# A decoder layer in split precision: position biases folded into a scale, the side branch's loads moved behind other copies, the last tile cut elsewhere, a shorter reciprocal root

## The chip, the core and the metric

One core of a Trainium2 chip runs the whole kernel. TensorE (PE) multiplies matrices and transposes; VectorE (DVE), ScalarE (ACT) and GpSimd (POOL) do the elementwise work; SyncE (SP) issues most transfers. The metric is the device time of one execution in microseconds.

## The reference

One hybrid layer on 512 tokens of width 1024, all in float32: block-sparse attention with position slopes (8 heads of 64) beside chunked retention (4 heads of 128), a gated feed-forward part with a convolution over three tokens, a side branch of `p` (width 256) under a gate, and a last norm. With 512 tokens there are two blocks of 256 keys and every earlier block is chosen, so the attention is plain causal attention.

```python
def rmsnorm(x, g):
    ms = jnp.mean(x * x, axis=-1, keepdims=True)
    return x * lax.rsqrt(ms + RMS_EPS) * g
...
h = rmsnorm(x, attn_norm[i])
mq, mk, mv, rq, rk, rv, rg = jnp.split(h @ w_in[i], split_points, axis=-1)
moba_out = ...   # softmax(q k^T * 64**-0.5 - 2**-(head+1) * distance) v, causal
ret_out = head_groupnorm(ret, ret_norm[i]) * jax.nn.silu(rg)
x = x + jnp.concatenate([moba_out, ret_out], axis=-1) @ w_out[i]
h = rmsnorm(x, ffn_norm[i])
u = causal_dwconv(h @ w_up[i], conv_w[i], conv_b[i])
x = x + (jax.nn.gelu(u) * (h @ w_gate[i])) @ w_down[i]
g = jax.nn.sigmoid(rmsnorm(x, ple_norm[i]) @ w_ple_gate[i])
x = x + (p[i] @ w_ple[i]) * g
return rmsnorm(x, final_norm)
```

## The kernel before

**Products.** Each float32 product is made from three (`mm3`, L91 to L95): both factors are split into a rounded part (`...h`) and the rest (`...l`), and high × high, high × low and low × high add up in one accumulator. The moving side has 512 columns nearly everywhere. Tiles of 128 × 512 come from a heap of 76 buffers (`h2k`), so a new tile can be made to wait for the last reader of an old one.

**Weights.** The SP queue loads blocks of 1 MB into one of two buffers `wr` (`fetch`, L125 to L134). `prepare` has ScalarE write the high part `wh` (L152) and VectorE or, for the weights of the projections and of the output product, POOL subtract to the rest `wl` (L154). It runs one part ahead of the products that use it (`need`).

**Order.** TensorE's instructions run in the order in which the code issues them (L846 to L853 add a dependence from each to the next). The order on the other engines is set by a scheduler of the framework.

**Stages.** The first norm and the retention values (to 34 us); projections and retention (to about 157 us); the attention loop (L646 to L671, to about 262 us); the feed-forward part (to 654 us); the last stage (to 701 us).

**The attention loop.** Heads are taken in pairs `g`, and each pair in two blocks of queries `b`. `moba_scores` makes the scores `ms` in PSUM and calls `softmax`: VectorE adds the bias and finds the least value (`ml`, L458), ScalarE takes the exponential with its sum (`me`, `mt`, L461), VectorE the reciprocal (`mi`), and one of them scales. `moba_turn` transposes the probabilities (`mp`), and ScalarE and VectorE split them into `corner` or `mph` and `mpl` (L515, L516). `moba_values` multiplies by the values (`mo`, L525 and L526), with small steps `mr`, `mt`, `mxh` behind it. Projections, halves of the output product (`ou`) and products of the side branch (`pw`) fill the gaps (`fills`). The heads of the query and key projections `mq` and `mk` are moved to their partitions by transfers from SBUF to SBUF, here called the copies (L380 and L389).

**The side branch.** `ple_load` (L572 to L580) issues four loads `wpr` of `w_ple` and two `pn` of `p`, 256 KB each; `ple_weights` (L589 to L594) splits the weights, with `wpl` on POOL.

**Roots.** `rsqrt_of` (L238 to L256) makes a reciprocal root on VectorE by an integer shift and three Newton steps. It is used for the norms (`r1`, `rr`, `r2`, `r3`: four columns) and for each of the last tiles (`r4`: one column).

**The last stage.** Gate weights are split into `wgh` and `wgl` by VectorE. For each half `c` of the columns and each tile `t` of 128 tokens come the gate product `pg` (24 products of 512 columns), and in `finish` (L788 to L803) the sigmoid `sg`, its product `sm` with `pw`, the residual sum `x`, the square with its sum (`fsq`, `fm`) and the product `x3n` with the last norm's weights on POOL. In the second half the root `r4` and the output `o` follow (L828 to L843). The last tile is cut in two parts of columns, and its `o` is made with the norm's weights in one step.

## Time and profile before

| | us |
|---|---|
| median of three runs | 699.3 (698.32 to 701.1) |
| the profiled execution | 702.57 |
| its span, first to last instruction | 700.8 |

Busy in that span: TensorE 682.7 us (97%), VectorE 428.2 (61%), ScalarE 291.1 (42%), POOL 124.3 (18%). Matmuls are pipelined, so their recorded durations overlap; the distance from one start to the next is what a product costs. In a timeline the figure in square brackets is the idle time of that engine just before the instruction, with what ended it. The mean granted clock is 0.997 of full speed.

### The profile page before, as it was taken

The numbers are of one execution on the slowest core, as the hardware profiler recorded it, in microseconds if no ns is written. First come the engines' busy times: TensorE is split into PE (matmuls) and PEld (weight loads), VectorE is DVE, ScalarE is ACT, GpSimd is POOL, SyncE is SP. The second block draws the span as 40 slices with busy tenths as digits, with TensorE's granted clock in tenths as the row PEclk, the third lists the DMA queues.
The fourth block names the chain that finished last, engine by engine and source line by source line (L and its number), as shares of the span: only waits on it lengthen the run. The fifth ranks groups of instructions, "written<-read, shape, count | busy, mean of one in ns | idle before, by whom it ended". The sixth has DMA issues, their size and how long they took to land.

```text
span 700.8 us, 8440 instructions
## 1 busy us (share of the span) xinstructions
PE 682.7 (97%) x3200; PEld 568.7 (81%) x3200; DVE 428.2 (61%) x769; ACT 291.1 (42%) x476; POOL 124.3 (18%) x99
## 2 busy tenths in 40 slices
PE   8999999999989999999999999999999999999995
PEld 6888888888777878888888888888888888888884
DVE  4676677766657656775656653234565565466496
ACT  4525543326657864453433431222343343344311
POOL 5145344334515210000000000000000000000145
PEclk9999999999999999999999999999999999999998
DMA  8245342236764011232331222233323212344003
GB/s 258 107 120 135 95 117 75 61 92 178 222 180 110 1 62 61 62 119 77 104 121 61 90 90 91 91 120 121 101 79 121 73 63 75 115 149 158 1 1 120
DMA packets 73390, 71.38 MB, mean 102 GB/s; under 512 B 2450, under 2 KB 62726, under 8 KB 73350
## 3 DMA queue, kind: packets, MB, share of 16 engines
q1 hardware_dynamic: 73190, 70.58, 33.3%
q8 instruction: 25, 0.41, 0.3%
q10 hardware_dynamic: 160, 0.27, 0.1%
q14 instruction: 15, 0.12, 0.1%
HBM read 62.97 MB, written 2.10 MB: 93 GB/s over the span
## 4 chain that ended last, share of the span: by engine, by line
PE 89%; DVE 4%; DMA 3%; ACT 1%; issue 1%; POOL 1%; SPq 0%; DVEq 0%; ACTq 0%; POOLq 0%
PE gate L93 6%; PE gate L94 6%; PE up L94 6%; PE dn L93 6%; PE dn L94 6%; PE gate L95 6%; PE up L95 6%; PE up L93 6%; PE dn L95 6%; PE pj L93 4%; PE pj L94 4%; PE pj L95 4%; PE ou L93 2%; PE ou L94 2%; PE ou L95 2%; PE pg L94 1%
## 5 line engine op out<-in xcount | busy, mean ns | idle before, releaser
L152 ACT ACTIVATE wh<-wr 128x1024 fp32r<-128x1024 f32 (+2 forms) x108 | 105.2, 979 | 204.5 <-PE dn L94 60.1
L154 DVE TENSOR_TENSOR wl<-wr,wh 128x1024 fp32r<-128x1024 f32 (+2 forms) x78 | 84.6, 1086 | 45.0 <-ACT wh L152 44.9
L154 POOL TENSOR_TENSOR wl<-wr,wh 128x1024 fp32r<-128x1024 f32 x30 | 73.3, 2444 | 129.9 <-ACT wh L152 129.8
L93 PE MATMUL gate<-h2h,wh 128*128 128x512 f32 x176 | 68.7, 390 | 0.0
L95 PE MATMUL gate<-h2h,wl 128*128 128x512 f32 x176 | 68.5, 389 | 0.0
L94 PE MATMUL gate<-h2l,wh 128*128 128x512 f32 x176 | 68.5, 389 | 0.0
L93 PE MATMUL up<-h2h,wh 128*128 128x512 f32 x176 | 68.5, 389 | 0.0
L94 PE MATMUL up<-h2l,wh 128*128 128x512 f32 x176 | 68.5, 389 | 0.0
L95 PE MATMUL up<-h2h,wl 128*128 128x512 f32 x176 | 68.5, 389 | 0.0
L93 PE MATMUL dn<-ach,wh 128*128 128x512 f32 x176 | 68.5, 389 | 0.0
L94 PE MATMUL dn<-acl,wh 128*128 128x512 f32 x176 | 68.5, 389 | 0.0
L95 PE MATMUL dn<-ach,wl 128*128 128x512 f32 x176 | 68.5, 389 | 0.0
L93 PE MATMUL pj<-h1h,wh 128*128 128x512 f32 x160 | 63.4, 396 | 1.1 <-DVE ml L458 0.9
L95 PE MATMUL pj<-h1h,wl 128*128 128x512 f32 x160 | 62.4, 390 | 0.0
L94 PE MATMUL pj<-h1l,wh 128*128 128x512 f32 x160 | 62.4, 390 | 0.0
L714 POOL MEMSET u<- 128x2 f32 x22 | 2.1, 99 | 316.9 <-DVE c L721 316.9
L725 DVE TENSOR_TENSOR ga<-gate,r2b 128x512 f32<-128x512 f32 x22 | 15.2, 691 | 41.3 <-PE gate L95 41.3
L715 DVE TENSOR_TENSOR u<-up,r2b 128x512 f32<-128x512 f32 x22 | 15.1, 691 | 40.1 <-PE up L95 40.1
L93 PEld LDWEIGHTS up<-h2h,wh 128*128 128x128 f32 x176 | 33.0, 188 | 6.9
L95 PEld LDWEIGHTS dn<-ach,wl 128*128 128x128 f32 x176 | 33.0, 188 | 6.9
L93 PEld LDWEIGHTS dn<-ach,wh 128*128 128x128 f32 x176 | 33.0, 188 | 6.9
L95 PEld LDWEIGHTS gate<-h2h,wl 128*128 128x128 f32 x176 | 33.0, 188 | 6.9
(235 smaller groups left out, 1416.8 us busy)
## 6 DMA issues: line engine op xcount, KB each, us to landing
wr<-in_w_up_dram SPq DMA_DIRECT2D x11, 1024.0 KB, 5.3
wr<-in_w_gate_dram SPq DMA_DIRECT2D x11, 1024.0 KB, 5.3
wr<-in_w_in_dram SPq DMA_DIRECT2D x20, 512.0 KB, 4.0
wr<-in_w_down_dram SPq DMA_DIRECT2D x8, 768.0 KB, 4.2
wr<-in_w_down_dram SPq DMA_DIRECT2D x8, 640.0 KB, 4.1
wr<-in_w_ple_gate_dram SPq DMA_DIRECT2D x4, 1024.0 KB, 5.2
wr<-in_w_out_dram SPq DMA_DIRECT2D x3, 1024.0 KB, 6.2
xn<-in_x_dram SPq DMA_DIRECT2D x8, 256.0 KB, 6.0
```

The costliest lines, as they stand in the source:

```text
L93: nc.tensor.matmul(acc, a[0], b[0], start=first, stop=False)
L94: nc.tensor.matmul(acc, a[0], b[1], start=False, stop=False)
L95: nc.tensor.matmul(acc, a[1], b[0], start=False, stop=last)
L152: nc.scalar.activation(hi, part, AF.Copy)
L154: (nc.gpsimd if aside else nc.vector).tensor_tensor(lo, part, f(hi), op=ALU.subtract)
L714: nc.gpsimd.memset(u[:, 0:2], 0.0)
L715: nc.vector.tensor_tensor(u[:, 2:], up, r2b, op=ALU.mult)
L725: nc.vector.tensor_tensor(ga, gate, r2b, op=ALU.mult)
```

## The change

It has five parts. Line numbers of the changed kernel are a little higher: L154, L156, L398, L407, L475, L479, L524, L542, L585, L588 and L602 are L152, L154, L380, L389, L461, L465, L515, L533, L576, L579 and L593 of before.

1. The eight tiles `bias` made by POOL are gone. The query heads are scaled by a column `qscale` that holds 64**-0.5 × 2**(h+1), and `softmax` reads the unscaled `base` and multiplies the sum by −2**−(h+1).
2. `ple_load` is issued at the end of step 2 of the loop, no longer at the end of step 1, and behind the last SP instruction; `ple_weights` is issued ahead of `moba_values` in its step.
3. The last tile is cut at column 384 where it was cut at 256.
4. `x3n` is made by VectorE.
5. The root takes nine instructions for four columns where it took twelve, and seven for one column where it took nine.

```diff
     def rsqrt_of(v, n, s):
-        sh = sm(s + "s", n, I32)
-        nc.vector.tensor_scalar(sh, v.bitcast(I32), 1, None, op0=ALU.logical_shift_right)
+        c = 1.5 ** 0.2
+        a = c ** (1 / 3)
         half = sm(s + "f", n)
         nc.vector.tensor_scalar(half, v, -0.5, None, op0=ALU.mult)
         y0 = sm(s + "y", n, I32)
-        nc.vector.tensor_scalar(y0, sh, -1.0, float(0x5F3759DF), op0=ALU.mult, op1=ALU.add)
-        y = y0.bitcast(F32)
-        for i in range(3):
+        nc.vector.tensor_scalar(y0, v.bitcast(I32), -0.5, float(0x5F3759DF) + math.log2(a) * 2 ** 23, op0=ALU.mult,
+                                op1=ALU.add)
+
+        def square(y):
             t = sm(s + "t", n)
...
-            y2 = sm(s + "y", n)
-            nc.vector.scalar_tensor_tensor(y2, t, 1.5, y, op0=ALU.add, op1=ALU.mult)
-            y = y2
-        return y
+            return t
+
+        y = y0.bitcast(F32)
+        t = square(y)
+        y1 = sm(s + "y", n)
+        nc.vector.scalar_tensor_tensor(y1, t, 1.5 * a ** 2, y, op0=ALU.add, op1=ALU.mult)
+        t = square(y1)
+        w = sm(s + "t", n)
+        nc.vector.scalar_tensor_tensor(w, t, 5 / 3 * c ** 2, t, op0=ALU.add, op1=ALU.mult)
+        y2 = sm(s + "y", n)
+        nc.vector.scalar_tensor_tensor(y2, w, 1.25 * c ** 4, y1, op0=ALU.add, op1=ALU.mult)
+        return y2
...
+    qscale = const.tile([P, HM // 2], F32, name="qscale")
+    for h in range(HM):
+        nc.gpsimd.memset(qscale[h % 2 * DH:(h % 2 + 1) * DH, h // 2:h // 2 + 1], DH ** -0.5 * 2.0 ** (h + 1))
...
-        nc.vector.scalar_tensor_tensor(t, acc, DH ** -0.5 if name == "mq" else 1.0, r1b, op0=ALU.mult, op1=ALU.mult)
+        nc.vector.scalar_tensor_tensor(t, acc, qscale[:, i:i + 1] if name == "mq" else 1.0, r1b, op0=ALU.mult,
+                                       op1=ALU.mult)
...
-    def moba_bias(h):
-        biases[h] = h2k("bias")
-        nc.gpsimd.tensor_scalar(biases[h], base, 2.0 ** -(h + 1), None, op0=ALU.mult)
...
-        nc.vector.tensor_tensor_reduce(e, s[:, :keys], biases[h][:, T - keys:], scale=-1.0,
+        nc.vector.tensor_tensor_reduce(e, s[:, :keys], base[:, T - keys:], scale=-2.0 ** -(h + 1),
                                        scalar=3.4e38, op0=ALU.add, op1=ALU.min, accum_out=least)
...
+        if 3 <= i < 7:
+            ple_weights((i - 3) // 2, (i - 3) % 2)
         if i >= 2:
             moba_values((i - 2) // 2, i % 2)
...
-        if i == 1:
-            ple_load()
-        if 3 <= i < 7:
-            ple_weights((i - 3) // 2, (i - 3) % 2)
+        if i == 2:
+            with tc.issue_after(last_of(mybir.EngineType.SP)):
+                ple_load()
...
-            nc.gpsimd.tensor_tensor(yn, y, fn[c], op=ALU.mult)
+            nc.vector.tensor_tensor(yn, y, fn[c], op=ALU.mult)
...
-            cuts = [(0, 256), (256, T)] if (t, c) == (NT - 1, 1) else [(0, T)]
+            cuts = [(0, 384), (384, T)] if (t, c) == (NT - 1, 1) else [(0, T)]
```

The change also moves instructions that it doesn't name. A name's number only tells buffers apart.

The SP queue in the attention loop, before, about 177 to 190 us: `wr` of the output product, key copies `mk`, the side branch's six loads, `wr`; the query copies `mq` come behind these.

```order
L115 DMA wr_2110<-in_w_out_dram 128x4x512
L389 DMA mk_9_1755<-mkh_1751 64x512 x2
L389 DMA mk_10_1756<-mkh_1751 64x512 x2
L389 DMA mk_11_1757<-mkl_1753 64x512 x2
L389 DMA mk_12_1758<-mkl_1753 64x512 x2
L576 DMA wpr_1827<-in_w_ple_dram 128x512
L576 DMA wpr_1829<-in_w_ple_dram 128x512
L576 DMA wpr_1831<-in_w_ple_dram 128x512
L576 DMA wpr_1833<-in_w_ple_dram 128x512
L579 DMA pn_1835<-in_p_dram 128x2x256
L579 DMA pn_1837<-in_p_dram 128x2x256
L115 DMA wr_2336<-in_w_out_dram 128x4x512
```

The same place after. The six loads have gone behind the query copies, and the two `wr` stand side by side.

```order
L117 DMA wr_2086<-in_w_out_dram 128x4x512
L117 DMA wr_2304<-in_w_out_dram 128x4x512
L398 DMA mq_5_1852<-mqh_1854 64x512
L398 DMA mq_6_1853<-mqh_1854 64x512
L398 DMA mq_5_1852<-mql_1856 64x512
L398 DMA mq_6_1853<-mql_1856 64x512
L585 DMA wpr_1946<-in_w_ple_dram 128x512
L585 DMA wpr_1948<-in_w_ple_dram 128x512
L585 DMA wpr_1950<-in_w_ple_dram 128x512
L585 DMA wpr_1952<-in_w_ple_dram 128x512
L588 DMA pn_1954<-in_p_dram 128x2x256
L588 DMA pn_1956<-in_p_dram 128x2x256
```

ScalarE in the same stretch, before, about 189 to 199 us, with the semaphores that each instruction waits for (`DMAHW` are queues of transfers; numbers 6 and 7 of `mph` are those of the query copies).

```order
L152 ACTIVATE wh_2116<-wr_2110 128x1024 [waits DMAHW6_49,PE_49,Pool_49]
L461 ACTIVATE me_1839,mt_1906<-me_1839,ml_1904 128x256 [waits DVE_49]
L515 ACTIVATE corner_606<-mp_1971 128x384 [waits PE_49]
L533 ACTIVATE mr_1933<-mo_1922 64x256
L461 ACTIVATE me_1840,mt_1913<-me_1840,ml_1911 128x256 [waits DVE_49]
L533 ACTIVATE mr_1933<-mo_1922 64x256 [waits DVE_49]
L465 ACTIVATE me_1840<-me_1840,mi_1915 128x256 [waits DVE_49]
L535 ACTIVATE mxh_1931<-mt_1934 128x256 [waits DVE_49,PE_49]
L515 ACTIVATE mph_1948<-mp_1947 128x512 [waits DMAHW7_49,DMAHW6_49]
L515 ACTIVATE mph_1978<-mp_1977 128x512 [waits DVE_49]
```

After. The exponential `me` of 256 columns now stands ahead of the weight copy `wh`, and the first `mph` has no wait of its own; those of the second are on copies of key heads.

```order
L475 ACTIVATE me_1803,mt_1870<-me_1803,ml_1868 128x256 [waits DVE_49]
L154 ACTIVATE wh_2092<-wr_2086 128x1024 [waits DMAHW6_49,PE_49,Pool_49]
L542 ACTIVATE mr_1893<-mo_1882 64x256
L524 ACTIVATE corner_610<-mp_1931 128x384 [waits PE_49]
L475 ACTIVATE me_1804,mt_1877<-me_1804,ml_1875 128x256 [waits DVE_49]
L542 ACTIVATE mr_1893<-mo_1882 64x256 [waits DVE_49]
L479 ACTIVATE me_1804<-me_1804,mi_1879 128x256 [waits DVE_49]
L544 ACTIVATE mxh_1891<-mt_1894 128x256 [waits DVE_49]
L524 ACTIVATE mph_1908<-mp_1907 128x512
L524 ACTIVATE mph_1938<-mp_1937 128x512 [waits DMAHW4_49,DMAHW3_49,DMAHW5_49,DMAHW2_49,PE_49]
```

POOL's queue in the second half of the loop, before.

```order
L154 TENSOR_TENSOR wl_2476<-wr_2336,wh_2475 128x1024
L453 TENSOR_SCALAR bias_2233<-base_419 128x512
L453 TENSOR_SCALAR bias_2235<-base_419 128x512
L154 TENSOR_TENSOR wl_2769<-wr_2336,wh_2768 128x1024
L593 TENSOR_TENSOR wpl_2303<-wpr_1829,wph_2301 128x512
L154 TENSOR_TENSOR wl_2818<-wr_2766,wh_2817 128x1024
L593 TENSOR_TENSOR wpl_2451<-wpr_1831,wph_2449 128x512
L154 TENSOR_TENSOR wl_2876<-wr_2766,wh_2875 128x1024
L593 TENSOR_TENSOR wpl_2598<-wpr_1833,wph_2596 128x512
```

After. Each `wpl` stands nearer the front, and the last one ahead of the last `wl`.

```order
L156 TENSOR_TENSOR wl_2307<-wr_2086,wh_2306 128x1024
L602 TENSOR_TENSOR wpl_2053<-wpr_1946,wph_2051 128x512
L156 TENSOR_TENSOR wl_2444<-wr_2304,wh_2443 128x1024
L602 TENSOR_TENSOR wpl_2207<-wpr_1948,wph_2205 128x512
L156 TENSOR_TENSOR wl_2737<-wr_2304,wh_2736 128x1024
L602 TENSOR_TENSOR wpl_2358<-wpr_1950,wph_2356 128x512
L156 TENSOR_TENSOR wl_2786<-wr_2734,wh_2785 128x1024
L602 TENSOR_TENSOR wpl_2493<-wpr_1952,wph_2491 128x512
L156 TENSOR_TENSOR wl_2844<-wr_2734,wh_2843 128x1024
```

VectorE at the last tile, before.

```order
L796 TENSOR_TENSOR sm_6077<-sg_6076,pw_2749 128x256
L797 TENSOR_TENSOR x_8_6079<-sm_6077,x2t_6021 128x256
L796 TENSOR_TENSOR sm_6077<-sg_6076,pw_2749 128x256
L799 ISA fsq_6078,fm_6084<-x_8_6079,fm_5822 128x256
L799 ISA fm_6084 128x1
L797 TENSOR_TENSOR x_8_6079<-sm_6077,x2t_6021 128x256
L799 ISA fsq_6078,fm_6088<-x_8_6079,fm_6084 128x256
L799 ISA fm_6088 128x1
L240 TENSOR_SCALAR r4s_6092<-fm_6088 128x1
L242 TENSOR_SCALAR r4f_6094<-fm_6088 128x1
```

After. The first part's steps are done together, and its square no longer stands between the steps of the second.

```order
L803 TENSOR_TENSOR sm_6023<-sg_6022,pw_2717 128x384
L804 TENSOR_TENSOR x_8_6025<-sm_6023,x2t_5967 128x384
L806 ISA fsq_6024,fm_6030<-x_8_6025,fm_5780 128x384
L806 ISA fm_6030 128x1
L803 TENSOR_TENSOR sm_6023<-sg_6022,pw_2717 128x128
L804 TENSOR_TENSOR x_8_6025<-sm_6023,x2t_5967 128x128
L806 ISA fsq_6024,fm_6034<-x_8_6025,fm_6030 128x128
L806 ISA fm_6034 128x1
L246 TENSOR_SCALAR r4f_6038<-fm_6034 128x1
L248 TENSOR_SCALAR r4y_6040<-fm_6034 128x1
```

## Rows read from the trace of the kernel before

**Rows 1.** The table of stretches: time, busy time of each engine, TensorE's clock, DMA.
```profile
150.00:260.00 110.00, 103.31 (x550) 86.81 (x549) 71.77 (x198) 71.95 (x161) 40.53 (x21) 1.00 0.45 126
300.00:650.00 350.00, 350.00 (x1548) 289.87 (x1547) 189.23 (x243) 125.10 (x164) 1.99 (x20) 1.00 0.31 99
```

**Rows 2.** TensorE's timeline: start, duration, work, idle time before it and its releaser.
```profile
191.02 0.50 PE L93 MATMUL pj<-h1h,wh 128*128 128x512 f32 x1 [0.89 <-DVE ml L458]
...
199.99 0.39 PE L525 MATMUL mo<-corner,mv 128*128 128x256 f32 x1 [2.32 <-DVE mpl L516]
...
221.28 0.50 PE L93 MATMUL ou<-mxh,wh 128*128 128x512 f32 x1 [1.70 <-DVE corner L516]
...
247.67 0.50 PE L94 MATMUL pw<-wpl,pTh 128*128 128x512 f32 x1 [0.85 <-POOL wpl L593]
...
255.53 0.39 PE L526 MATMUL mo<-corner,mv 128*128 128x256 f32 x1 [0.21 <-DVE corner L516]
```

**Rows 3.** The SP queue's timeline, 185 to 190 us: issue times of transfers.
```profile
185.21 1.77 SPq L576 DMA_DIRECT2D wpr<-in_w_ple_dram  x4
...
188.60 1.11 SPq L380 DMA_DIRECT2D mq<-mqh  x2
```

**Rows 4.** ScalarE's timeline, 188 to 199 us.
```profile
188.91 1.04 ACT L152 ACTIVATE wh<-wr 128x1024 fp32r<-128x1024 f32 x1
189.85 0.49 ACT L461 ACTIVATE me<-me,ml 128x256 f32<-128x256 f32 x1
...
198.62 1.08 ACT L515 ACTIVATE mph<-mp 128x512 fp32r<-128x512 f32 x2 [3.81 <-DMA mq<-mqh]
```

**Rows 5.** The chain that ended last, 189 to 199 us: start, length, what.
```profile
189.12 9.41 DMA mq<-mqh
```

**Rows 6.** POOL's and VectorE's timeline at 154 us.
```profile
153.89 2.40 POOL L154 TENSOR_TENSOR wl<-wr,wh 128x1024 fp32r<-128x1024 f32 x1 [5.45 <-ACT wh L152]
153.91 2.40 DVE L240 TENSOR_SCALAR rrs<-rrv 128x4 int32<-128x4 int32 x1
```

**Rows 7.** POOL's timeline, 243 to 248 us.
```profile
243.90 2.41 POOL L154 TENSOR_TENSOR wl<-wr,wh 128x1024 fp32r<-128x1024 f32 x1 [7.07 <-ACT wh L152]
246.35 1.27 POOL L593 TENSOR_TENSOR wpl<-wpr,wph 128x512 fp32r<-128x512 f32 x1
```

**Rows 8.** TensorE, narrow products: timeline of the last tile and at 188 us, chain at 153.
```profile
152.90 0.80 PE rcs L269 x8
...
188.51 0.93 PE L513 MATMUL mp<-ident,me 128*128 128x128 f32 x7
...
690.38 0.28 PE L95 MATMUL pg<-wgh,h3l 128*128 128x256 f32 x1
690.50 0.28 PE L93 MATMUL pg<-wgh,h3h 128*128 128x256 f32 x1
```

**Rows 9.** The last stage: timelines of VectorE, POOL (three rows), TensorE.
```profile
661.52 2.38 DVE L82 TENSOR_TENSOR wgl<-wr,wgh 128x512 fp32r<-128x512 f32 x2
...
660.95 1.80 POOL L803 TENSOR_TENSOR x3n<-x,fn 128x512 f32<-128x512 f32 x1 [94.42 <-DVE x L797]
665.43 1.73 POOL L803 TENSOR_TENSOR x3n<-x,fn 128x512 f32<-128x512 f32 x1 [2.69 <-DVE x L797]
...
691.72 3.17 POOL L832 TENSOR_SCALAR o<-x3n,r4y 128x512 f32<-128x512 f32 x2 [1.27 <-issue]
...
672.19 0.50 PE L94 MATMUL pg<-wgl,h3h 128*128 128x512 f32 x1 [0.16 <-DVE wgl L82]
```

**Rows 10.** The last chain: timelines of ScalarE and VectorE.
```profile
692.13 0.47 ACT L794 ACTIVATE sg<-pg,r3y 128x256 f32<-128x256 f32 x1 [2.40 <-PE pg L95]
...
692.64 0.42 DVE L796 TENSOR_TENSOR sm<-sg,pw 128x256 f32<-128x256 f32 x1 [0.22 <-ACT sg L794]
...
694.48 0.15 DVE L240 TENSOR_SCALAR r4s<-fm 128x1 int32<-128x1 int32 x1
...
696.20 0.88 DVE L837 SCALAR_TENSOR_TENSOR o<-x,r4y,fn 128x256 f32<-128x256 f32 x2
```

More of the change, by code (lines that the diff above doesn't have):

```diff
@@ L1 @@
 from contextlib import ExitStack
+import math
 import numpy as np
@@ L446, in ret_gate @@
         mix[MW // P + h] = split(t2, "mx")
-    biases, probs, probsT, pair = {}, {}, {}, {}
-    def moba_bias(h):
-        biases[h] = h2k("bias")
-        nc.gpsimd.tensor_scalar(biases[h], base, 2.0 ** -(h + 1), None, op0=ALU.mult)
+    probs, probsT, pair = {}, {}, {}
     def softmax(s, h, qt, e):
@@ L493, in moba_scores @@
             del qs["mq", g], qs["mk", g], pair[g]
-            for e in range(2):
-                del biases[2 * g + e]
-        elif g + 1 < HM // 2:
-            for e in range(2):
-                moba_bias(2 * g + 2 + e)
     def moba_turn(g, b, e):
@@ L631, in hybrid_layer_kernel @@
         project(*tiles[3 * h + 2])
-        if h == 1:
-            for e in range(2):
-                moba_bias(e)
     big = [lambda n=n, h=h: project(n, h) for n, h in feature_tiles[15:]]
```

## The prediction

> **What bounds the kernel now.** I read the table of stretches first [rows 1]. From 300 to 650 us TensorE is busy for the whole 350.00 us, in 1548 recorded products, or 0.226 us for one of 512 columns. No edit touches that stretch, so its time stays. From 150 to 260 us it is busy for 103.31 of 110.00: 6.7 us are lost in the attention loop. The reader should look there, and at the end, where the chain after the last product is bare. Next came TensorE's timeline, for the idle time in square brackets and the engine that ended it [rows 2]. Five stalls, of 0.89, 2.32, 1.70, 0.85 and 0.21 us, make 5.97 of the 6.7; two short ones at 160 and 207 us are touched by no edit, and I leave them. A bracket counts from the modelled end of the product before. A product lasts 0.39 to 0.40 us and the next starts 0.226 after it, so a stall costs its bracket and 0.16 more: 1.05, 2.48, 1.86, 1.01 and 0.37. Then I followed each releaser back on its own engine.
>
> **The stall at 200 us.** The chain of waits has a DMA here, the copy of a query head, 9.41 us long, landing at 198.53 [rows 5]. ScalarE's `mph` waits for it, idle for 3.81 us [rows 4], though it doesn't read the head: the order of before names the queues of those copies, whose buffer `mph` takes over. The copies are issued at 188.60, behind the six loads of `w_ple` and `p`, 1.5 MB from 185.21 on [rows 3], and a 1 MB `wr`. In the changed order this `mph` waits for no DMA, the one after it for copies of key heads that left a loop step earlier, and the six loads stand behind the query copies. What is late next is VectorE's `mpl`. Without the wait `mph` starts at 198.62 − 3.81 = 194.81, and the product followed it by 1.37, which gives 196.18; TensorE has work until 197.67. So all 2.48 go, with 1.5 us to spare.
>
> **The stall at 191 us.** TensorE waits for a scores' buffer, which VectorE's minimum holds, and that waits in turn on the exponentials. ScalarE takes the weight copy `wh` first, 1.04 us, and starts an exponential of 0.49 at 189.85 when it ends [rows 4]. The change turns the two round: the exponential comes 1.04 earlier, and 1.05 goes to nothing or 0.1. The weight copy comes 0.49 later; weights are prepared a part ahead, 24 products or 5.4 us, which hides it, and without that cover it would cost its 0.49.
>
> **The stalls at 248 and 256 us.** `wpl` stands in POOL's queue behind a `wl` of 2.41 us and starts as that ends [rows 7]. In the changed order the last two change places, and the biases ahead are gone. A `wl` that now stands behind a `wpl` comes 1.27 later; the part ahead hides that too, and it costs 1.27 once if not. So the 1.01 goes. The 0.37 is a corner of the probabilities that waits behind ScalarE's other work, and a corner now stands ahead there: gone.
>
> **The stall at 221 us** stays but for its share of VectorE, whose minimum reads `base` and no longer a bias that POOL is writing beside it. I take 0.35 off, the middle of 0 and 0.7.
>
> The loop gives 1.05 + 2.48 + 1.01 + 0.37 + 0.35 = 5.26 us. Against it stand waits that no row shows: each DMA also waits for the eighth before it, the last `wr` for POOL's `wl`, and the six loads land later. I put 0.6 against it, between 0 and 2.5 (one stall of the largest size), and keep **4.7 us**.
>
> **Edits at nothing.** The eight biases were POOL work beside a busy TensorE. The eight `memset` lie under the first loads. The column in place of a constant adds no instruction. The shorter root takes three VectorE instructions from each root of four columns, and most of that is no gain: `rrs` lasts 2.40 us because POOL's `wl`, 2.40 too, starts 0.02 before it and ends with it [rows 6]. With `rrs` gone the next operation stands in the same place and takes the 2.40. I take 0.1 us for all roots but the last, between 0 and 0.5.
>
> The SBUF page of the Trainium skill ("SBUF — State Buffer", section "Who interferes with whom") has a rule for such a pair: VectorE and GpSimd share a pair of ports under an exclusive lock, whoever comes first keeps it for the whole instruction, and the other blocks. The two rows of 2.40 agree with it.
>
> **The last stage.** POOL's `x3n`, 1.80 us, lies beside VectorE's two `wgl`, which take 2.38 together [rows 9]. On VectorE an `x3n` costs about 0.6: a two-input step of 256 columns takes 0.42 [rows 10], so one of 512 lies between 0.42 and 0.84. The same price makes a `wgl` pair 1.2 when POOL is still. The step from one `x3n` to the next, 660.95 to 665.43, is 4.5 us [rows 9]; it becomes 4.5 + 0.6 − 1.2 = 3.9, and TensorE's wait for `wgl` at 672 us, 0.16 + 0.16 [rows 9], goes: 0.3. If the pair stays at 2.38, the step is 5.1 (a rival below).
>
> By the rule of the same SBUF page `x3n` on VectorE, which reads two SBUF tiles, would be blocked by POOL's `o`, 3.17 us for two [rows 9], so by up to 1.6 us each time. The trace speaks against it: `sm` reads two SBUF tiles as well and takes its 0.42 at 692.64 [rows 10], inside the pair of `o` that starts at 691.72 [rows 9]. By the rule the sum would lose nothing on TensorE either, as the 5 us of the last tile's products lie beside it.
>
> **The last tile** was 48 products of 256 columns, 0.12 apart [rows 8]: 5.76 us. It is now 24 of 384 and 24 of 128. For 384 I take the middle of 0.120 and 0.226: 24 × 0.173 = 4.15. For 128 there is no row: no product of this type is narrower than 256, and the code widens even 128-key scores to 256. The nearest rows:
> - The line through 512 and 256 goes on to 0.067: 24 × 0.067 = 1.6, sum 5.75, no change.
> - Transposes of 128 columns, seven in 0.93 us [rows 8], at most 0.13 each: 3.1, sum 7.3, 1.5 more.
> - The column sums, four products as eight instructions in 0.80 us, 0.20 for a product although it has one column [rows 8]: 4.8, sum 8.95, 3.2 more.
>
> I choose 0.20: of the rows under 256 columns it is the one of products and not of transposes, and a price that doesn't fall with the columns is what the widened scores suggest. The ends, 0 and 3.9 (a narrow product at the 0.226 of a wide one), stay in the range.
>
> Then comes the bare chain: ScalarE's sigmoid at 692.13, VectorE's `sm`, `x`, square and root, `o` at 696.20 [rows 10]. The last part has 128 columns now and not 256. The sigmoid loses some 0.1 of 0.47, and the three VectorE steps 0.12 each, between 0 and half of 0.42: 0.47. The first part's square, which stood among them by the order, is ahead now: 0.25, between 0 and 0.48. The root took 694.48 to 696.20 for nine instructions, 0.19 each; two fewer are 0.38. Together **1.1 us**. At the end this makes 3.2 − 1.1 − 0.3 = **1.8 us more**, or 1.4 less where narrow products cost 0.067.
>
> **Sum:** −4.7 − 0.1 + 1.8 = −3.0 us. The profiled execution took 702.6 us (span 700.8), 3.3 above the median of the three runs, 699.3. The stalls were read in that longer execution and may be smaller in the runs; I take the gain whole from the median: **696.3 us**.
>
> **Rivals.**
> - *Narrow products are cheap* (0.067 to 0.13): the end gives −1.4 to +0.1, the whole −6.2 to −4.7, 693.1 to 694.6, say 694. For it: 512 to 256 columns halves the price. Against: the widened scores, and the 0.20 for one column.
> - *The waits only move.* The query copies still follow eight copies of key heads and two `wr` of 1 MB, or a `wl` comes late behind a `wpl`. The loop gives 1.5 in place of 4.7: 699.5.
> - *Slower: VectorE bounds the last stage.* The `wgl` pair stays at 2.38 beside `x3n`, by another stretch. Four steps of 0.6 more are 2.4 us on TensorE, where a wait for `wgl` exists already; the end is then 3.2 − 1.1 + 2.4 = 4.5 more. It is slower as soon as the loop gives under 4.5: with 1.5, 702.3, with nothing, 703.8. For it: that wait. Against: the stretch has its POOL row beside it, and that row goes.
>
> The TensorE page of the Trainium skill ("TensorE: Matmul & The Clock Gate", section "Back-to-back issue gap") gives some 81 ns for a product of 128 columns in a stream with weight loads. By it, as an estimate, the 24 take 1.9 us and the first rival holds. Its 131 ns for 512 columns is not this trace's 226, so I give it little weight.
>
> **How the numbers follow.** Forecast 0.50, cheap narrow products 0.29, waits only moved 0.13, slower 0.08. A measurement of this kernel can tell 0.5%, 3.5 us, from no change: faster is under 695.8, slower over 702.8. The forecast spreads by some 1.3 us either way, so 0.16 of its chance lies under 695.8; with 0.27 of the first rival, faster has 0.43. Of the last rival 0.05 lies over 702.8, and 0.52 is left. The range goes from the cheap case to the third, 693.3 to 699.8; the largest gains of the first and the slower case stay outside, under 2 in 10.
>
> **What would show it.** In the changed profile: on TensorE no idle time over 0.2 us from 189 to 201, and no DMA in the chain there; the last tile's products 0.17 and 0.20 apart; `wgl` pairs of about 1.2 us; seven root instructions, 1.3 us, ahead of the last `o`. I am wrong if narrow products stand 0.07 to 0.13 apart (2 us too high), or if TensorE waits for a `wl`, `mpl` or `wgl` by over 0.5 us at a new place (too low).

## The result and the profile after

| | before | after |
|---|---|---|
| median of eight runs, us | 700.62 (698.32 to 703.36) | 696.09 (694.34 to 697.10) |
| ratio to before | 1 | 0.9924 (95% interval 0.9906 to 0.9942) |
| span of the profiled execution, us | 700.8 | 692.6 |

The kernel became 4.1 to 6.6 us faster by the interval, 4.5 by the medians. The profiled executions differ by 8.2 us, but 1.9 of that lies ahead of the first weight product, where the change does nothing that TensorE waits for. Two rows of TensorE's timeline show it, the first of before and the second of after: the first `mv` product.

```profile
33.99 0.48 PE L93 MATMUL mv<-wh,h1h 128*128 128x512 f32 x1
```

```profile
32.07 0.47 PE L95 MATMUL mv<-wh,h1h 128*128 128x512 f32 x1
```

In the fourteen traces of this study that product starts between 31.8 and 34.0 us whatever the kernel (31.8 in one that starts exactly as before does, 33.2 in one that starts as the changed one does), so it is scatter between executions. The other 6.3 us lie behind that product. A second trace of the changed kernel has 5.4 there, so they carry about 1 us of scatter too. The table of stretches of the changed kernel (time, busy time of PE, PEld, DVE, ACT and POOL, clock, DMA share, GB/s) shows where, beside [rows 1]:

```profile
150.00:260.00 110.00, 107.83 (x582) 91.93 (x582) 73.39 (x198) 73.35 (x164) 31.55 (x15) 1.00 0.44 122
300.00:650.00 350.00, 350.00 (x1554) 290.31 (x1553) 184.96 (x246) 119.98 (x158) 1.88 (x19) 1.00 0.31 98
```

In the loop TensorE now loses 2.17 us where it lost 6.69; from 300 to 650 us nothing changed. Of the five stalls of [rows 2] one is left, on TensorE's timeline of the changed kernel:

```profile
214.99 0.50 PE L95 MATMUL ou<-mxh,wh 128*128 128x512 f32 x1 [1.33 <-DVE corner L525]
```

It answers to the one at 221 us and is 1.33 where that was 1.70. The other four are gone, 1.05 + 2.48 + 1.01 + 0.37 by the prediction's count; with the 0.37 that the fifth lost this makes 5.3 us. Some tenths come on top, since the first product behind each stall is slower.

ScalarE's timeline of the changed kernel answers to [rows 4]: the exponential stands ahead of the weight copy, and `mph` waits for nothing that is late.

```profile
185.99 0.51 ACT L475 ACTIVATE me<-me,ml 128x256 f32<-128x256 f32 x1
186.56 1.06 ACT L154 ACTIVATE wh<-wr 128x1024 fp32r<-128x1024 f32 x1
...
190.24 1.07 ACT L524 ACTIVATE mph<-mp 128x512 fp32r<-128x512 f32 x2
```

The last stage, VectorE's timeline, answers to [rows 9] and [rows 10]:

```profile
653.36 0.69 DVE L810 TENSOR_TENSOR x3n<-x,fn 128x512 f32<-128x512 f32 x1
653.96 1.28 DVE L84 TENSOR_TENSOR wgl<-wr,wgh 128x512 fp32r<-128x512 f32 x2
...
657.30 0.69 DVE L810 TENSOR_TENSOR x3n<-x,fn 128x512 f32<-128x512 f32 x1
...
685.51 0.29 DVE L803 TENSOR_TENSOR sm<-sg,pw 128x128 f32<-128x128 f32 x1
...
686.62 0.15 DVE L246 TENSOR_SCALAR r4f<-fm 128x1 f32<-128x1 f32 x1
...
687.96 0.88 DVE L844 SCALAR_TENSOR_TENSOR o<-x,r4y,fn 128x256 f32<-128x256 f32 x2
```

The `wgl` pair takes 1.28 us where it took 2.38, and the step from one `x3n` to the next 3.94 (653.36 to 657.30) where it took 4.48; TensorE no longer waits for a `wgl`. The root takes 1.34 us (686.62 to 687.96), the `sm` of 128 columns 0.29.

On TensorE the last tile answers to [rows 8]; these are two products of 384 columns and two of 128:

```profile
681.93 0.33 PE L96 MATMUL pg<-wgl,h3h 128*128 128x384 f32 x1
682.11 0.34 PE L97 MATMUL pg<-wgh,h3l 128*128 128x384 f32 x1
...
683.12 0.28 PE L97 MATMUL pg<-wgh,h3l 128*128 128x128 f32 x1
683.23 0.27 PE L95 MATMUL pg<-wgh,h3h 128*128 128x128 f32 x1
```

They stand 0.17 to 0.18 and 0.11 us apart. The price of the narrow product is where the prediction missed.

### The profile page after: what moved, and what is told of

It reads as the page before. It is cut to its first block, busy times and chain, and to the rows that moved or that the text cites. A ratio compares the mean times of both kernels' runs of the same rounds, so it can differ in the third digit from the quotient of the medians.

```text
span 692.6 us, 8399 instructions
## 1 busy us (share of the span) xinstructions
PE 680.9 (98%) x3200; PEld 569.5 (82%) x3200; DVE 421.5 (61%) x747; ACT 291.0 (42%) x476; POOL 102.9 (15%) x92
## 4 chain that ended last, share of the span: by engine, by line
PE 94%; DVE 2%; ACT 1%; DMA 1%; issue 0%; SPq 0%; DVEq 0%; ACTq 0%
PE gate L95 6%; PE gate L96 6%; PE dn L95 6%; PE up L96 6%; PE dn L96 6%; PE gate L97 6%; PE up L97 6%; PE up L95 6%; PE dn L97 6%; PE pj L95 5%; PE pj L96 5%; PE pj L97 5%; PE pg L97 2%; PE pg L95 2%; PE pg L96 2%; PE ou L97 2%
## 5 line engine op out<-in xcount | busy, mean ns | idle before, releaser
L154 ACT ACTIVATE wh<-wr 128x1024 fp32r<-128x1024 f32 (+2 forms) x108 | 105.2, 979 | 206.4 <-PE dn L96 60.2
L156 DVE TENSOR_TENSOR wl<-wr,wh 128x1024 fp32r<-128x1024 f32 (+2 forms) x78 | 84.6, 1086 | 45.2 <-ACT wh L154 45.1
L156 POOL TENSOR_TENSOR wl<-wr,wh 128x1024 fp32r<-128x1024 f32 x30 | 73.4, 2447 | 122.4 <-ACT wh L154 114.7
```

Source lines behind the costliest of these rows:

```text
L154: nc.scalar.activation(hi, part, AF.Copy)
L156: (nc.gpsimd if aside else nc.vector).tensor_tensor(lo, part, f(hi), op=ALU.subtract)
```

## The experiments

Each ratio is against the kernel before, run beside it on the same chip; the interval is of 95%. A time in us is a median.

**The buffer of `mph` alone.** The kernel before, with a spare tile that takes the buffer which `mph` had.

```diff
             for kp in range(b, -1, -1):
                 tp = ps("mp")
+                if (g, b, e) == (0, 1, 0) and kp < b:
+                    nc.gpsimd.memset(h2k("pad")[:, :1], 0.0)
                 hi, lo = corner[e] if kp == b else (h2k("mph", F32R), h2k("mpl", F32R))
```

> The kernel before with one edit: a spare tile is taken from the heap just before the first `mph` of the loop, so that `mph` gets another buffer and waits for no transfer; the loads of the side branch stay ahead of the query copies. Theory 1 (the late copies stopped TensorE through the reused buffer): the stall at 200 us goes, 2.0 to 2.5 us, and the ones at 191, 221, 248 stay; time 0.9965 to 0.997 of before, some 698. Rival (the copies are late themselves, and the next reader of the query heads waits): the stall moves a few us on and the time stays within 0.3 us.

Measured: 1.0020 (1.0003 to 1.0038), 702.5 us. Neither theory's time came. The timelines of ScalarE, VectorE and TensorE of this kernel say why:

```profile
192.47 0.58 ACT L517 ACTIVATE mph<-mp 128x512 fp32r<-128x512 f32 x1
```

```profile
196.23 0.69 DVE L518 TENSOR_TENSOR mpl<-mp,mph 128x512 fp32r<-128x512 f32 x1 [3.20 <-DMA mq<-mql]
```

```profile
196.97 0.39 PE L527 MATMUL mo<-corner,mv 128*128 128x256 f32 x1 [1.55 <-DVE mpl L518]
```

`mph` starts at 192.47 and waits for no copy. But the buffers moved on by one, and now VectorE's `mpl` takes over the buffer of another half of the query head, waits 3.20 us for the copy of `mql`, and TensorE stands for 1.55 where it stood for 2.32. The wait changed its place, by the same mechanism: the buffers of `mqh` and of `mql` both hang on these copies, and the spare tile takes only one of them.

The time is even 0.2 to 2.7 us above that of before. Behind the stall at 218.78 us (1.71 in brackets) the trace has something that the trace of before lacks. The granted clock falls to 0.50, the lower of TensorE's two levels (1.2 GHz), from 219.6 to 223.0 us, and products of 512 columns stand 0.43 apart in place of 0.23. A row of the table of stretches (the clock is the number ahead of the last two) and two of TensorE's timeline:

```profile
219.60:222.90 3.30, 3.30 (x9) 2.59 (x8) 3.18 (x6) 2.01 (x5) 1.32 (x2) 0.50 0.64 198
```

```profile
220.83 0.63 PE L93 MATMUL ou<-mxh,wh 128*128 128x512 f32 x1
221.26 0.63 PE L94 MATMUL ou<-mxl,wh 128*128 128x512 f32 x1
```

This costs 1.6 us in that execution (nine products in 3.64 us in place of 2.05), more than the shorter wait gave. The mean clock of the timed runs, 0.9939 here and 0.9950 in those of before, fits, but how often it fell in them is not shown.

**The loads' place alone undone.** The changed kernel, with the loads again ahead of the query copies.

```diff
-        if 3 <= i < 7:
-            ple_weights((i - 3) // 2, (i - 3) % 2)
         if i >= 2:
             moba_values((i - 2) // 2, i % 2)
...
-        if i == 2:
-            with tc.issue_after(last_of(mybir.EngineType.SP)):
-                ple_load()
+        if i == 1:
+            ple_load()
+        if 3 <= i < 7:
+            ple_weights((i - 3) // 2, (i - 3) % 2)
```

> The changed kernel with part 2 alone undone: the six loads are issued at the end of step 1 again, ahead of the query copies, and the weights split behind `moba_values`. In this build the first `mph` waits for no transfer. Theory 1 (place of the loads matters only through the buffer of `mph`): no stall over 0.5 us at 190 to 200; the `wpl` stall of about 1.0 us comes back if `wpl` is again behind a `wl`; time 0 to 1.5 us over the changed kernel. Rival (the copies that come late stop the loop): a stall of 2 to 2.5 us there again, time 2.5 to 4 us over the changed kernel.

Measured: 0.9925 (0.9904 to 0.9946), 696.1 us, the time of the changed kernel. The SP queue's timeline, the transfers of `mq` from issue to landing (least, middle, most) and ScalarE's timeline:

```profile
181.96 2.77 SPq L585 DMA_DIRECT2D wpr<-in_w_ple_dram  x4
...
186.98 1.13 SPq L398 DMA_DIRECT2D mq<-mqh  x2
```

```profile
DMA to landing us min/median/max: 8.0/8.0/8.1
```

```profile
190.71 1.07 ACT L524 ACTIVATE mph<-mp 128x512 fp32r<-128x512 f32 x2
```

The copies stand behind the loads again and land 8.0 us behind their issue (9.4 before), so at 195 us. `mph` starts at 190.71 all the same, since it has another buffer in this build, and TensorE has no stall from 185 to 200. A late copy costs nothing as long as nobody waits for it: the stall at 200 us was the reuse of a buffer, and the loads can only have decided how long it lasted. The `wpl` stall is back, as theory 1 has it, in TensorE's timeline:

```profile
240.94 0.50 PE L96 MATMUL pw<-wpl,pTh 128*128 128x512 f32 x1 [0.85 <-POOL wpl L602]
```

The one at 256 us is back with it (0.20 in brackets), and the one at 215 us is 0.68 where the changed kernel has 1.33, which I had not expected. In the stretch from 150 to 260 us TensorE is busy for 107.26 us, 0.57 less than in the changed kernel, too little for the times.

**The loads' place alone done.** The kernel before, with the diff above turned round.

```diff
+        if 3 <= i < 7:
+            ple_weights((i - 3) // 2, (i - 3) % 2)
         if i >= 2:
...
+        if i == 2:
+            with tc.issue_after(last_of(mybir.EngineType.SP)):
+                ple_load()
```

> The kernel before with part 2 alone. My sum gives it the stalls at 200 (2.48) and 248 us (1.01): 3.5 us faster than before, 0.995. The stalls at 191 (1.05) and 221 (1.86) stay, since the biases stay. Rival (what the change gained is mostly the biases'): under 2 us.

Measured: 0.9959 (0.9942 to 0.9977), 2.9 us faster by the ratio and 2.0 by the medians. The table of stretches, TensorE's timeline, and the timelines of the SP queue and of ScalarE:

```profile
150.00:260.00 110.00, 106.83 (x563) 90.36 (x562) 75.39 (x199) 72.13 (x161) 40.43 (x21) 0.98 0.45 126
```

```profile
190.83 0.50 PE L93 MATMUL pj<-h1h,wh 128*128 128x512 f32 x1 [0.82 <-DVE ml L458]
...
218.47 0.50 PE L93 MATMUL ou<-mxh,wh 128*128 128x512 f32 x1 [1.32 <-DVE corner L516]
```

```profile
188.49 1.10 SPq L380 DMA_DIRECT2D mq<-mqh  x2
```

```profile
194.54 1.07 ACT L515 ACTIVATE mph<-mp 128x512 fp32r<-128x512 f32 x2
```

TensorE is busy for 3.52 us more in the loop. That this is the sum's 3.5 is chance: the stalls at 200, 248 and also 256 us are gone, the one at 191 stays, the one at 221 is 1.32 where it should have stayed whole, and a new wait of 0.32 stands at 216.5. Behind that pair the clock falls to 0.50 here too (from 219.0 to 222.4 us; the table has 0.98 as the mean), which costs 1.6 us. The copies leave at 188.49, no earlier than the 188.60 of before, and `mph` waits for none of them: it is the other buffer again. Done alone the part gives 2.9 us; undone alone it costs nothing that the times can tell. Both builds have other buffers than before, and either frees `mph`; the parts do not add up.

**The biases back.** The changed kernel with POOL's eight biases, the constant scale and `softmax` as before.

```diff
+                moba_bias(2 * g + 2 + e)
...
-        nc.vector.tensor_tensor_reduce(e, s[:, :keys], base[:, T - keys:], scale=-2.0 ** -(h + 1),
+        nc.vector.tensor_tensor_reduce(e, s[:, :keys], biases[h][:, T - keys:], scale=-1.0,
```

> The changed kernel with part 1 alone undone: POOL makes the eight biases again. In this build ScalarE takes the weight copy ahead of the exponential at 191 us again. My sum: the stall of 1.05 there is back, the one at 215 us is longer by 0.35, the rest as in the changed kernel: 1.4 us over the changed kernel, 0.9945 of before. Rival (biases are hidden on POOL): no stall there, 0 to 0.3 us over.

Measured: 0.9943 (0.9921 to 0.9964), 697.0 us, 1.0 over the changed kernel by the medians and 1.3 by the ratios. ScalarE's and TensorE's timelines and the table of stretches:

```profile
186.67 1.04 ACT L154 ACTIVATE wh<-wr 128x1024 fp32r<-128x1024 f32 x1
...
187.91 0.49 ACT L479 ACTIVATE me<-me,ml 128x256 f32<-128x256 f32 x1
```

```profile
189.08 0.50 PE L95 MATMUL pj<-h1h,wh 128*128 128x512 f32 x1 [0.82 <-DVE ml L476]
```

```profile
150.00:260.00 110.00, 106.74 (x575) 90.36 (x575) 73.75 (x196) 72.31 (x162) 40.54 (x21) 1.00 0.44 122
```

The weight copy is ahead of the exponential again, and TensorE waits 0.82 us as at 191 before; it is busy for 1.09 us less in the loop. The stall at 215 us is not one longer wait but three shorter ones, of 0.30, 0.80 and 0.56 in brackets, together 0.33 more. So what the biases' removal gives is in the main an order on another engine, which nothing in the diff names. The times alone (the intervals overlap) would not show it.

**The last tile cut at 256 again.** The changed kernel with the cut of before.

```diff
-            cuts = [(0, 384), (384, T)] if (t, c) == (NT - 1, 1) else [(0, T)]
+            cuts = [(0, 256), (256, T)] if (t, c) == (NT - 1, 1) else [(0, T)]
```

> The changed kernel with part 3 alone undone: the last tile is cut at 256 again. By the prediction (a 128-column product costs 0.20 us): products 5.76 us in place of 8.95, chain 0.8 longer, so 2.4 us faster than the changed kernel. By what the changed kernel's trace shows (128 columns 0.111 apart): products 5.76 in place of 6.85, the chain from the last product to the last `o` 4.0 in place of 3.2, so 0.3 us faster, which the times can't tell.

Measured: 0.9923 (0.9899 to 0.9947), 696.0 us against 696.1. The prediction's 2.4 us are not there. VectorE's timeline shows what eats the 0.3:

```profile
685.37 0.82 DVE L803 TENSOR_TENSOR sm<-sg,pw 128x256 f32<-128x256 f32 x1 [1.03 <-ACT sg L801]
```

This is the last `sm`, 256 columns, which took 0.42 before [rows 10]. POOL's second `o` of a pair starts just ahead of it (the pair runs from 683.65 for 3.14 us, so its half is at 685.2). In the run below that has this `o` on ScalarE, the same `sm` takes 0.42.

**The last tile cut at 448.** The changed kernel with a narrower last part.

```diff
-            cuts = [(0, 384), (384, T)] if (t, c) == (NT - 1, 1) else [(0, T)]
+            cuts = [(0, 448), (448, T)] if (t, c) == (NT - 1, 1) else [(0, T)]
```

> The changed kernel with the last tile cut at 448, to price a 64-column product. Theory A (a floor of about 0.11 us for one product, whatever its columns): 0.11 apart, products 4.8 + 2.7 = 7.5 us, chain 0.25 shorter than the changed kernel's, time 0.3 to 0.4 us over it. Theory B (cost follows the columns): 0.06 apart, products 6.2 us, time 0.9 us under it. The prediction's theory (0.20 however narrow) gives 9.6 us.

Measured: 0.9924 (0.9897 to 0.9952), 696.1 us. TensorE's timeline, three products of 64 columns:

```profile
686.06 0.28 PE L97 MATMUL pg<-wgh,h3l 128*128 128x64 f32 x1
686.17 0.28 PE L95 MATMUL pg<-wgh,h3h 128*128 128x64 f32 x1
686.28 0.28 PE L96 MATMUL pg<-wgl,h3h 128*128 128x64 f32 x1
```

0.11 apart, as with 128 columns. Theory A holds: a product with its weight load has a floor of 0.11 us, and 256 columns at 0.12 stand just above it. The times of the cuts can't be told apart.

**`x3n` on POOL again.** The changed kernel with part 4 undone.

```diff
-            nc.vector.tensor_tensor(yn, y, fn[c], op=ALU.mult)
+            nc.gpsimd.tensor_tensor(yn, y, fn[c], op=ALU.mult)
```

> The changed kernel with part 4 alone undone: `x3n` on POOL again. My theory: each `wgl` pair beside an `x3n` lasts 2.4 us again where it takes 1.28 now, TensorE waits 0.3 us for a `wgl` in the last stage, and the time is 0.3 us over the changed kernel. Rival (the stretch comes from the scalar engine or from memory, not from POOL): pairs stay at 1.3 us, no wait, same time.

Measured: 0.9917 (0.9894 to 0.9940), 695.8 us. POOL's, VectorE's and TensorE's timelines:

```profile
654.65 1.79 POOL L810 TENSOR_TENSOR x3n<-x,fn 128x512 f32<-128x512 f32 x1 [93.89 <-DVE x L804]
```

```profile
655.22 2.37 DVE L84 TENSOR_TENSOR wgl<-wr,wgh 128x512 fp32r<-128x512 f32 x2
```

```profile
666.25 0.50 PE L96 MATMUL pg<-wgl,h3h 128*128 128x512 f32 x1
```

The pair lasts 2.37 again beside `x3n`, and the products at 666 us start 0.39 and 0.34 apart in place of 0.226: 0.28 us of waiting. The mechanism is as I had it, and its worth is under what the times can tell.

**A weight copy moved.** The changed kernel, with the `wh` at 212 us behind the second `mph` of its turn.

```diff
                 nc.scalar.activation(hi[:, c0:], tp[:, c0:], AF.Copy)
+                if (g, b, e, kp) == (1, 1, 1, 0):
+                    anchor.append(last_of(mybir.EngineType.Activation))
...
+                if key == ("out", 0, 1):
+                    with tc.issue_after(anchor[0]):
+                        nc.scalar.activation(hi, part, AF.Copy)
+                else:
+                    nc.scalar.activation(hi, part, AF.Copy)
```

> The changed kernel with one weight copy moved: the `wh` of 1.05 us that ScalarE takes at 212.4 us, ahead of the corner that TensorE waits for at 215, is put behind the second `mph` of that turn, six instructions later. Theory (the stall of 1.48 us at 215 us is that copy's place in ScalarE's queue): the stall falls to 0.4 or 0.5 us, time 1.0 us under the changed kernel, some 0.991 of before. Rival (something else is late just as long, VectorE's steps or the loads): the stall stays over 1 us and the time is the same.

Measured: 0.9907 (0.9885 to 0.9930), 694.7 us. The timelines of TensorE and VectorE:

```profile
215.78 0.50 PE L95 MATMUL ou<-mxh,wh 128*128 128x512 f32 x1 [0.67 <-DVE corner L533]
```

```profile
214.85 0.41 DVE L551 TENSOR_TENSOR mt<-mo,mr 64x256 f32<-64x256 f32 x1
215.19 0.54 DVE L533 TENSOR_TENSOR corner<-mp,corner 128x384 fp32r<-128x384 f32 x1
```

The stall fell from 1.33 to 0.67 in brackets, 0.66 us, two thirds of the 1.0 expected. With ScalarE's copy away, VectorE's `mt` of 0.41 stands ahead of the corner: the next late thing on the next engine. The time can't be told from the changed kernel's.

**Again the changed kernel**, beside the three kernels that follow.

> The changed kernel itself again, so that it stands beside the other kernels of this call on the same chip: 0.9924 of before, 0.990 to 0.9945; TensorE idle about 2.2 us from 150 to 260 us, with the one long stall near 215 us.

Measured: 0.9909 (0.9883 to 0.9935), 695.7 us, as expected; by the medians it is 6.0 us under before, where the first measurement had 4.5.

**Two edits on top.** The changed kernel with the weight copy moved, the cut at 256, and the `o` of the tile before the last on ScalarE, issued behind the last tile's first sigmoid.

```diff
-            cuts = [(0, 384), (384, T)] if (t, c) == (NT - 1, 1) else [(0, T)]
+            cuts = [(0, 256), (256, T)] if (t, c) == (NT - 1, 1) else [(0, T)]
...
             finish(t, c, accs, xt, cuts)
+            for dst, src, root in late:
+                nc.scalar.activation(dst, src, AF.Copy, scale=root)
...
+            if t == NT - 2:
+                late += [(o[i], x3[t, i], r4) for i in range(2)]
+                continue
```

> The changed kernel with two more edits: the weight copy of 212 us behind the second `mph` (as in the run before: the stall at 215 us 0.83 in place of 1.48), and the last tile cut at 256 again with the `o` of the tile before it on ScalarE, issued behind the last tile's first sigmoid, in place of POOL. Theory (128 columns cost nearly what 256 do, and a POOL `o` that starts beside VectorE's `sm` stretches it by 0.3 to 0.4): last products 5.8 us in place of 6.9, the chain to the last `o` 3.7 in place of 3.2, total 1.2 us under the changed kernel, 0.9905 of before. Rival (ScalarE's two `o` delay the last sigmoid): the chain takes 4.4 or more and the kernel is at most 0.6 under the changed one.

Measured: 0.9889 (0.9866 to 0.9912), 694.2 us, 1.5 under the changed kernel beside it by the medians. The intervals still overlap, so that it beats the changed kernel is likely and not shown. The chain took 4.1 us, between the theory and the rival, from the last product to the last `o`. The timelines of ScalarE, TensorE and VectorE:

```profile
683.21 1.33 ACT L842 ACTIVATE o<-x3n,r4y 128x512 f32<-128x512 f32 x2 [1.57 <-DVE r4y L274]
684.45 0.45 ACT L809 ACTIVATE sg<-pg,r3y 128x256 f32<-128x256 f32 x1
```

```profile
683.72 0.28 PE L97 MATMUL pg<-wgh,h3l 128*128 128x256 f32 x1
```

```profile
687.79 0.88 DVE L861 SCALAR_TENSOR_TENSOR o<-x,r4y,fn 128x256 f32<-128x256 f32 x2
```

The two `o` end at 684.5, and the last sigmoid, whose products are done at 684.0, waits for them.

**The last stage alone.** The kernel before with parts 3, 4 and 5; the new root is the one of the change's diff.

```diff
-            nc.gpsimd.tensor_tensor(yn, y, fn[c], op=ALU.mult)
+            nc.vector.tensor_tensor(yn, y, fn[c], op=ALU.mult)
...
-            cuts = [(0, 256), (256, T)] if (t, c) == (NT - 1, 1) else [(0, T)]
+            cuts = [(0, 384), (384, T)] if (t, c) == (NT - 1, 1) else [(0, T)]
```

> The kernel before with parts 3, 4 and 5 alone (cut at 384, `x3n` on VectorE, shorter root); loads and biases as before. By my sum the loop's five stalls stay whole, and the last stage is 1.8 us longer if a narrow product costs 0.20. By the trace of the changed kernel the last stage gives 1.1 more products, 1.2 less chain and 0.3 less wait: 0.4 us faster than before, 0.9994.

Measured: 1.0000 (0.9982 to 1.0019), 701.8 us. TensorE's timeline has the stall of 200 us as before:

```profile
199.30 0.38 PE L537 MATMUL mo<-corner,mv 128*128 128x256 f32 x1 [2.30 <-DVE mpl L528]
```

What the times can tell of the change comes from the loop: 0.4 us is far under this interval of 1.3 us either way. The trace has the shorter end, 3.17 us from the last product to the last `o` as in the changed kernel. It also has a low clock behind the stall at 199 us (0.50 from 201 to 204 us): from that product to TensorE's next wait it takes 8.3 us, where the trace of before takes 6.8.

**The old root.** The changed kernel with the shift and the three equal steps of before.

```diff
+        sh = sm(s + "s", n, I32)
+        nc.vector.tensor_scalar(sh, v.bitcast(I32), 1, None, op0=ALU.logical_shift_right)
...
+        for i in range(3):
```

> The changed kernel with part 5 alone undone (twelve and nine instructions for a root). My sum: 0.38 us more in the last chain and 0.1 elsewhere, 0.5 us over the changed kernel. Rival (the loop waits for the longer retention roots too): an added wait on TensorE at 155 to 170 us and over 1 us in all.

Measured: 0.9903 (0.9880 to 0.9927), 695.0 us, no slower than the changed kernel. VectorE's timeline, the first instruction of the last root and the `o` behind it:

```profile
689.10 0.15 DVE L242 TENSOR_SCALAR r4s<-fm 128x1 int32<-128x1 int32 x1
...
690.83 0.88 DVE L833 SCALAR_TENSOR_TENSOR o<-x,r4y,fn 128x256 f32<-128x256 f32 x2
```

The root takes 1.73 us against 1.34: the 0.39 is there and is under the scatter of the times. There is no wait at 155 to 170 us that the changed kernel lacks.

## Why the prediction was right, and where not

The predicted 696.3 us and the measured 696.1 agree better than the steps behind them. Part of it is luck: with more runs the median of before moved from 699.3 to 700.6, and the gain is 4.5 to 5.3 us, by medians and by the ratio, and 6.0 in the second measurement, and not 3.0. The forecast came out because it started from a median too low and took off too little.

**The loop: right in size.** The sum of 5.26 us was 5.3 in the trace, stall by stall. The 0.6 that I held back for new waits was not needed: no new place has a wait of 0.3 us or more. But its price of a stall, the bracket and 0.16, was read from a trace whose clock stayed at 1.00. In the traces of the three other kernels made from the one before the clock fell behind a stall, and that execution lost another 1.6 us or so. Whether the kernel before loses this in some of its runs, and the change with it saves more than its stalls, is not shown.

**The stall at 200 us: right that it goes, its cause half right.** I named the buffer and the place of the loads together. The runs tell them apart: with the loads early and the copies 8.0 us late there is no stall if `mph` and `mpl` have other buffers; with a spare tile in the old kernel the wait goes on to `mpl`. It is the buffer that stops TensorE. That the changed kernel gives these tiles other buffers is a by-product of what else allocates.

**191 us: right.** The order on ScalarE turns with the biases, and with them back the stall is back, 0.82 in brackets. **248 and 256 us: right**, with `wpl` back behind `wl` in one run (0.85 in brackets, as before) and the 256 one with it. **221 us: right in size**, 0.37 off where I took 0.35, but the biases are not shown to be its cause: the kernel of before with the loads moved keeps them and has the same 1.32, and the changed kernel with the loads early has 0.68. What sets its length stays open, but for the weight copy that half of it hangs on.

**The last tile: the step that failed.** I took 0.20 us for a 128-column product, from the column sums, against the rows of transposes, at most 0.13. It is 0.11. The 24 narrow products take 2.7 us in place of 4.8, the tile 6.8 in place of 8.95: 1.1 more than before, where I had 3.2. This one term was too dear by 2.1 us, about what the gain exceeds the forecast by. The rows had the right price: the column sums are eight instructions in 0.80 us, each with a weight load of its own, so 0.10 for one. I divided by the four products of the code, though a narrow `pg` is a single instruction. The seven transposes of [rows 8] take 0.68 us from the first start to that of the next instruction, 0.10 each; my 0.13 counted the modelled end of the last one in. The first rival had the price right, and the TensorE page of the Trainium skill ("TensorE: Matmul & The Clock Gate", section "Back-to-back issue gap") was nearer with its 81 ns than my row. But its smaller figure is not what this trace has either, 111 at 64 and at 128 columns. I read the widened scores of the code as a statement on the price, which no row was.

**The bare chain: right.** From the last product to the last `o` it was 4.38 us (691.82 to 696.20) and is 3.17 (684.79 to 687.96): 1.2 where I had 1.1. With 1.1 for the products and 0.3 for the `wgl` the last stage gives 0.4 us, where I had it lose 1.8; the run with these parts alone can't tell 0.4 from nothing.

**Roots: right**, 0.39 in the last and nothing that the times show elsewhere. **`x3n`: right**, 3.94 for the step where I had 3.9.

**The weighed rule was dismissed too soon.** I wrote that the trace speaks against a lock between VectorE and POOL's `o`, from an `sm` in the middle of one. In the changed kernel an `sm` that starts 0.25 us behind such an `o` is longer; see below.

## What to carry to other kernels

A tile that waits for a transfer it never reads waits for a buffer: look up who held it, and expect that any edit that allocates or frees something may free or bind it, so that such gains don't add up over the parts of a change. Ask of every engine's queue which instruction stands ahead of the one that TensorE waits for; here the stall at 191 us and half of the one at 215 were one weight copy each. Divide a busy time by the instructions of the trace and not by the operations of the code. A split that makes the last part of a tile narrower can pay only as long as a product's cost falls with its columns, here down to 256.

## What the hardware showed that I had not expected

**A product has a floor.** 512, 448, 384 and 256 columns stand 0.227, 0.20, 0.17 and 0.12 us apart; 128 and 64 both 0.11. Each of these has a weight load of its own (128 x 128), and the loads of the narrow products start 0.11 apart as well, so whether the floor is the product's or its load's is not shown. Cutting a tile at 384 thus costs 1.1 us of TensorE for a chain that is 0.8 shorter (1.2 less the root's 0.39).

**The clock can fall behind a stall.** In the traces of all three experiments made from the kernel before, the granted clock fell to 0.50 for 3.4 us. It fell 0.5 to 1.5 us after TensorE had taken up work again behind a stall of 1.3 to 2.3 us. In the trace of before it did not, behind stalls as long, nor in any of the ten traces of the changed kernel and its variants while products ran, with stalls of 1.33 us at most. So a stall can cost 1.6 us more than its bracket, but not each time; what decides it is not shown.

**A POOL instruction can hold VectorE for a part of its own length.** Before, `x3n` (two inputs) on POOL held VectorE's first `wgl` almost to its end [rows 9]. POOL's `o` (one tile and a column) does less. Two timelines, POOL's and VectorE's, of the changed kernel, and then of the one with the last stage alone:

```profile
682.84 3.10 POOL L839 TENSOR_SCALAR o<-x3n,r4y 128x512 f32<-128x512 f32 x2 [3.24 <-DVE r4y L268]
...
683.09 0.84 DVE L803 TENSOR_TENSOR sm<-sg,pw 128x384 f32<-128x384 f32 x1 [0.42 <-ACT sg L801]
```

```profile
690.88 3.10 POOL L844 TENSOR_SCALAR o<-x3n,r4y 128x512 f32<-128x512 f32 x2 [2.13 <-issue]
...
691.58 0.56 DVE L808 TENSOR_TENSOR sm<-sg,pw 128x384 f32<-128x384 f32 x1 [0.86 <-ACT sg L806]
```

The pair of `o` starts at 682.84 and `sm` at 683.09: it takes 0.84 us. Where `sm` comes 0.70 us behind the start of the `o`, it takes 0.56, as `x` of the same 384 columns does. The traces with the cut at 256 and with the old root agree: there `sm` is held until 0.54 or 0.55 us after an `o` has started, here until 0.53. So it looks as if the first half microsecond of the `o` is what blocks, about a third of its 1.56. The Trainium skill ("SBUF — State Buffer", section "Who interferes with whom") says that a VectorE instruction with two SBUF inputs contends with a GpSimd one that reads SBUF, and of VectorE's two-port modes that whoever issues first keeps the ports for the whole instruction. Taken for both, this agrees with the two-input `x3n` (a pair of 2.37 beside 1.79) and not with `o`. That the one-input form is the reason is a guess: no run varied it alone.
